# Column sums of a modulation vector: 32x32 block transpositions on VectorE and one matmul per section, in place of ones-matmuls per four columns

## The chip, the cores and the metric

The program runs on one core of a Trainium2 chip, in one launch. The metric is device time in microseconds (us), taken as the median of several executions. One more execution is profiled, and all rows below come from that one. TensorE is called PE here, VectorE DVE, ScalarE ACT, GpSimd POOL, and SyncE, which issues nearly all transfers, SP.

## What is computed

Two transformer-like blocks run one after the other on 512 tokens of width 1024, in float32. Each block makes a modulation vector of 6 sections of 1024 numbers from one condition vector; the sections scale, shift and gate the block's two halves:

```python
mod = (jax.nn.silu(c) @ w_ada[i] + b_ada[i])[:, None, :]
shift_m, scale_m, gate_m, shift_f, scale_f, gate_f = jnp.split(mod, N_MOD, axis=-1)
h = rmsnorm(x, norm_mix_w[i]) * (1.0 + scale_m) + shift_m
x = x + gate_m * hybrid_mixer(h, ...)        # chunked state-space scan, pooling branch, w_out
h = rmsnorm(x, norm_mlp_w[i]) * (1.0 + scale_f) + shift_f
x = x + gate_f * (jnp.square(jax.nn.relu(h @ w_up[i])) @ w_down[i])
...
mod = c_act @ w_ada[l] + b_ada[l]            # second block: six sections again
y = token_mixer(h, ...)                      # mLSTM heads beside banded attention
y = conv_ffn(h, ...)
```

So the modulation is two products of a vector of 1024 with a matrix of 1024 x 6144. Everything else is large products with 512 token rows, and the scan, attention and norms between them.

## The kernel before

**Large products.** Every weight matrix comes from memory in pieces of 128 x 1024 (tile `wraw`). ACT rounds a piece to its high part `whi` (L243), DVE forms the low part `wlo` (L244), and PE multiplies in three fp32r products, high by high, low by high and high by low, with 512 columns each (L274 into `ga`, L352 into `gb`). PE, DVE and ACT each work through one fixed list of instructions. A scheduler writes these lists when the program is built; it takes the order of the Python code as its priority and moves instructions within it. An instruction at the head of an engine's list that waits holds everything behind it.

**The modulation.** It is too thin for PE's large products, so DVE does it, spread over the whole run in small steps. `ada_steps` handles two columns of 128 outputs: two transfers of 512 KB each bring the weights, and eight DVE operations of 128 x 256 (L155, then seven of L157) multiply by the condition's value of each partition and add up into an accumulator `adacc`. What is left is the sum over the 128 partitions. `ada_sum` does this for four columns, that is two accumulators: four fp32 matmuls with a matrix of ones, each into 32 partitions of a PSUM tile `adaps` (L164, eight records in the trace, since an fp32 matmul shows as two), a copy by ACT to `colraw` (L167), a PE transposition (L170), and one DVE addition of the bias into `mod` (L171). Four sections of block 1 and six of block 2, two sums each: 20 such sums. (The first two sections of block 1 have code of their own, `first_mod`, L497 on: two accumulators for each of 8 columns, taken from the same ring of `ADB` buffers as `adacc`, matmuls L506, transposition L511, DVE L512.)

`ada_next` is one step of it. `pump` calls it between the other work at a rate that each stage sets, and `ada_until(block, section)` is called where a section is needed; it finishes what of it is missing. The vectors are needed at these places: (0,2) before the gate rows `gm`, (0,4) and (0,3) before the `w_out` product, (0,5) at the end of the first half of the `w_up` products, where `cols_to_rows` turns it into rows (PE transposition `rowps`, L216, ACT copy L218), (1,0) and (1,1) at the end of the second half, (1,2), (1,4) and (1,3) at the end of the attention and mLSTM stage, and (1,5) before the last `w_down` product (`g2_col`, again `rowps`).

**Stages, by the trace's time.** 0 to 70 us: first norms, `first_mod`, first columns of `w_in` (`h_tile`: `ntmp`, `hh`, `hl`, lines L424 to L433). 190 to 610 us: the state-space scan, where DVE and ACT do the decay tiles and the convolution between products. 650 to 675 us: the `w_out` product and the second norm, tile by tile. 675 to 1020 us: `w_up` and `w_down`. 1020 to 1260 us: mixer of block 2 (`ips`, L1430, and `hm`, L1448, belong to the mLSTM). After 1260 us: its feed-forward part.

## Time and profile before

| | |
|---|---|
| median of 3 executions | 1624.59 us (1624.26 to 1624.70) |
| the profiled execution | 1624.09 us |
| its span, first to last instruction | 1622.3 us |
| PE busy | 1589.5 us |
| DVE busy | 1086.5 us |
| ACT busy | 715.4 us |
| POOL busy | 28.3 us |

The span is what the trace covers; 1.8 us of the execution lie around it. Busy time is the sum of an engine's instructions. Matmuls overlap, so their durations can't be added up: what one costs PE is read from the distance between starts.

### The profile page before, as it was taken

Reading aid. Unit: us, or ns where it says so; the run is one execution under the profiler, and the core shown is the slowest. Engines: PE = TensorE matmul, PEld = TensorE weight load, DVE = VectorE, ACT = ScalarE, POOL = GpSimd, SP = SyncE. Lnnn points to the kernel's source line nnn. Section 1 sums busy time; section 2 is a strip of 40 time slices with the busy share of each in tenths; the row PEclk is TensorE's granted clock in tenths of the full one; section 3 lists DMA queues with packets and bytes.
Section 4 is the critical chain, followed back from the end, with each engine's and each line's share of the span. In section 5 each row is a group of like instructions: output and inputs, shape, how many; then the busy total and the mean of one; then the engine's idle time right before and its main releaser. Section 6 shows DMA issues by size and latency. Waiting matters only on the chain.

```text
span 1622.3 us, 20792 instructions
## 1 busy us (share of the span) xinstructions
PE 1589.5 (98%) x7810; PEld 1274.0 (79%) x7810; DVE 1086.5 (67%) x1995; ACT 715.4 (44%) x1275; POOL 28.3 (2%) x47
## 2 busy tenths in 40 slices
PE   5999999999999999999999999999999999999998
PEld 3778777777877878877877788887788888888886
DVE  6686897888766675876257773578876756145644
ACT  4543656555454332633214332655555643144421
POOL 0000000000000000000000000000011000000000
PEclk9999999999999999999999999999999999999999
DMA  9731544444444435466236571122331323332321
GB/s 280 197 100 59 178 142 149 130 143 138 149 130 138 142 127 177 137 196 209 96 115 197 195 252 48 53 81 76 94 102 53 103 81 102 91 104 87 96 91 53
DMA packets 206830, 206.45 MB, mean 127 GB/s; under 512 B 11469, under 2 KB 184585, under 8 KB 206729
## 3 DMA queue, kind: packets, MB, share of 16 engines
q1 hardware_dynamic: 206729, 205.12, 41.6%
q8 instruction: 61, 1.00, 0.3%
q14 instruction: 40, 0.33, 0.1%
HBM read 202.90 MB, written 2.19 MB: 126 GB/s over the span
## 4 chain that ended last, share of the span: by engine, by line
PE 90%; DVE 4%; DMA 3%; ACT 2%; issue 1%; SPq 0%; POOL 0%; DVEq 0%; POOLq 0%; ACTq 0%
PE ga L274 53%; PE gb L352 21%; PE gb L312 5%; PE go L1494 2%; PE ga L544 2%; DMA wraw<-in_w_ada_dram 1%; DMA AB<-acs 1%; DVE wlo L244 1%; PE nps L424 1%; PE yps L829 1%; PE stps L838 0%; ACT arel L803 0%; PE yps L834 0%; DMA x<-in_x_dram 0%; PE adaps L164 0%
## 5 line engine op out<-in xcount | busy, mean ns | idle before, releaser
L274 PE MATMUL ga<-hh,whi 128*128 128x512 f32 (+1 forms) x1200 | 464.6, 390 | 1.0 <-ACT hh L431 0.9
L244 DVE TENSOR_TENSOR wlo<-wraw,whi 128x1024 fp32r<-128x1024 f32 (+3 forms) x249 | 297.9, 1198 | 246.8 <-ACT whi L243 246.2
L274 PE MATMUL ga<-hl,whi 128*128 128x512 f32 (+1 forms) x1200 | 457.6, 382 | 2.2 <-DVE hl L433 2.1
L274 PE MATMUL ga<-hh,wlo 128*128 128x512 f32 (+1 forms) x1200 | 456.8, 382 | 0.0
L243 ACT ACTIVATE whi<-wraw 128x1024 fp32r<-128x1024 f32 (+3 forms) x249 | 257.5, 1036 | 335.3 <-PE gb L352 151.4
L274 PEld LDWEIGHTS ga<-hh,whi 128*128 128x128 f32 x1200 | 224.1, 188 | 54.1 <-issue 6.7
L274 PEld LDWEIGHTS ga<-hl,whi 128*128 128x128 f32 x1200 | 225.3, 188 | 50.6 <-issue 3.3
L274 PEld LDWEIGHTS ga<-hh,wlo 128*128 128x128 f32 x1200 | 225.3, 188 | 46.7
L157 DVE SCALAR_TENSOR_TENSOR adacc<-wraw,csil,adacc 128x256 f32<-128x256 f32 x280 | 133.7, 482 | 36.1 <-DMA wraw<-in_w_ada_dram 31.7
L352 PE MATMUL gb<-whi,hidh 128*128 128x512 f32 x240 | 78.2, 396 | 0.0
L352 PE MATMUL gb<-wlo,hidh 128*128 128x512 f32 x240 | 77.8, 394 | 0.0
L352 PE MATMUL gb<-whi,hidl 128*128 128x512 f32 x240 | 77.5, 394 | 0.0
L450 DVE SCALAR_TENSOR_TENSOR xs<-xraw,colB,xs 128x511 f32<-128x511 f32 (+2 forms) x72 | 53.8, 748 | 8.8 <-ACT xs L448 7.9
L352 PE MATMUL gb<-whi,fh 128*128 128x512 f32 x176 | 57.3, 396 | 0.0
L352 PE MATMUL gb<-wlo,fh 128*128 128x512 f32 x176 | 57.2, 395 | 0.0
L352 PE MATMUL gb<-whi,fl 128*128 128x512 f32 x176 | 57.0, 394 | 0.0
L352 PEld LDWEIGHTS gb<-whi,hidh 128*128 128x128 f32 x240 | 45.0, 188 | 10.8 <-issue 0.4
L803 ACT ACTIVATE arel<-AB,acs 128x128 f32<-128x128 f32 x128 | 40.7, 389 | 29.0 <-DMA AB<-acs 20.6
L352 PEld LDWEIGHTS gb<-whi,hidl 128*128 128x128 f32 x240 | 45.1, 188 | 10.7
L352 PEld LDWEIGHTS gb<-wlo,hidh 128*128 128x128 f32 x240 | 45.1, 188 | 10.4
L274 PE MATMUL ga<-yh,whi 128*128 128x512 f32 x128 | 51.1, 399 | 0.0
L274 PE MATMUL ga<-yh,wlo 128*128 128x512 f32 x128 | 50.6, 395 | 0.0
(421 smaller groups left out, 2374.2 us busy)
## 6 DMA issues: line engine op xcount, KB each, us to landing
wraw<-in_w_ada_dram SPq DMA_DIRECT2D x80, 512.0 KB
wraw<-in_w_in_dram SPq DMA_DIRECT2D x72, 512.0 KB
wraw<-in_w_down_dram SPq DMA_DIRECT2D x54, 512.0 KB
wraw<-in_w_up_dram SPq DMA_DIRECT2D x88, 256.0 KB
wraw<-in_w_up_dram SPq DMA_DIRECT2D x32, 512.0 KB
araw<-in_w_ada_dram SPq DMA_DIRECT2D x32, 256.0 KB
AB<-acs SPq DMA_DIRECT2D x32, 256.0 KB
wraw<-in_w_branch_ssd_dram SPq DMA_DIRECT2D x16, 512.0 KB
```

Of the source, the lines that this page charges most:

```text
L157: V.scalar_tensor_tensor(out=acc, in0=raw[:, k], scalar=s_, in1=acc, op0=ALU.mult, op1=ALU.add)
L243: act(out=hi, in_=raw, func=AF.Copy)
L244: V.tensor_tensor(out=lo, in0=raw, in1=f(hi), op=ALU.subtract)
L274: PE.matmul(ps[:, n0:n1], lhsT=a[:, m * P:(m + 1) * P], rhs=b[:, n0:n1], start=i == 0, stop=i == 3 * n - 1)
L312: PE.matmul(pss[t][:, 0:ncols], lhsT=a[:, t * P:(t + 1) * P], rhs=b, start=k == 0 and j == 0, stop=k == n - 1 and j == 2)
L352: PE.matmul(pss[t][q], lhsT=a, rhs=w[b][q], start=i == 0 and j == 0, stop=i == n - 1 and j == 2)
L424: PE.transpose(ps[:, i * P:(i + 1) * P], xh[t][j // 4][:, (j % 4) * P:(j % 4 + 1) * P], ident)
L450: V.scalar_tensor_tensor(out=o[:, d:], in0=ps[:, 0:S - d], scalar=cols[taps - 1 - d], in1=o[:, d:], op0=ALU.mult, op1=ALU.add)
L544: PE.matmul(fps[i], lhsT=a[:, i * P:(i + 1) * P], rhs=b, start=j == 0 and q == 0, stop=j == 7 and q == 2)
L803: act(out=t[:, i * P:(i + 1) * P], in_=AB[q][:, i * P:(i + 1) * P], func=AF.Relu, scale=-1.0, bias=acs[:, hh:hh + 1])
L829: PE.matmul(ps[r * 64:(r + 1) * 64, j * P:(j + 1) * P], lhsT=xdt[:, hh * 64:(hh + 1) * 64], rhs=M[hh // 4][:, (hh % 4) * P:(hh % 4 + 1) * ...
L1494: PE.matmul(opss[t][q], lhsT=x_, rhs=w[q][b_], start=half == 0 and k == 0 and j == 0, stop=half == 1 and k == 3 and j == 2)
```

## The change

The accumulator now holds four columns (128 x 512, a tile from the general pool `U` of 64 slots, no longer from the ring of `ADB`). When its 32 operations are done, DVE transposes it in blocks of 32 x 32 (L165, tile `adtr`) and sums each block's rows (L166), which leaves 16 numbers per partition in `adR`: the sums over each group of 32 partitions. When a section is needed, one fp32 matmul with a constant matrix `quarters` (four identity matrices of 32 in each direction) adds the four groups of partitions (L196). Three small DVE operations keep from the four results the one that belongs to each partition (L198, L201) and add the bias (L202). The PE transposition and ACT's copy are gone. `ADB`, now only the ring of `first_mod`, goes from 5 to 3. Two constants are made once. Line numbers above 206 become smaller by 8, those above 590 by 3.

```diff
--- before.py
+++ after.py
@@ -143,36 +143,32 @@
     mod = [const("mod1", [P, 48]), const("mod2", [P, 48])]
     ada_w, bcol = [w_ada, w_ada_2], [ba_col, None]
 
+    adR = [const("adR1", [P, 192]), const("adR2", [P, 192])]
     def ada_steps(ci, col):
 
-        acc = small("adacc", [P, 2 * P], bufs=ADB)
-        for k0 in (0, 4):
-            raw = RAW([P, 4, 2 * P])
-            dma(out=raw, in_=ada_w[ci][0, k0 * P:(k0 + 4) * P, col * P:(col + 2) * P].rearrange("(k p) n -> p k n", p=P))
-            for k in range(4):
-                s_ = csil[:, 8 * ci + k0 + k:8 * ci + k0 + k + 1]
-                if k0 + k == 0:
-                    V.tensor_scalar(out=acc, in0=raw[:, k], scalar1=s_, scalar2=None, op0=ALU.mult)
-                else:
-                    V.scalar_tensor_tensor(out=acc, in0=raw[:, k], scalar=s_, in1=acc, op0=ALU.mult, op1=ALU.add)
-            yield acc
-    def ada_sum(ci, col, accs):
-        ps = PS("adaps")
-        for j in range(4):
-            PE.matmul(ps[j * 32:(j + 1) * 32, 0:P], lhsT=ones[:, 0:32], rhs=accs[j // 2][:, j % 2 * P:(j % 2 + 1) * P],
-                      start=True, stop=True)
-        row = small("colraw", [P, P])
-        act(out=row, in_=ps[:, 0:P], func=AF.Copy)
-        yield
-        ps = PS("adaps")
-        PE.transpose(ps[:, 0:P], row, ident)
-        V.tensor_tensor(out=mod[ci][:, col:col + 4], in0=ps[:, 0:P:32], in1=bcol[ci][:, col:col + 4], op=ALU.add)
-        yield
-    ada_todo = [(0, 8 * sec + i) for sec in (2, 4, 3, 5) for i in range(0, 8, 2)] + [(1, i) for i in range(0, 48, 2)]
-    ada_now, ada_open, ada_half = [], [], []
+        acc = U("adacc")
+        for h in range(2):
+            a = acc[:, h * 2 * P:(h + 1) * 2 * P]
+            for k0 in (0, 4):
+                raw = RAW([P, 4, 2 * P])
+                dma(out=raw, in_=ada_w[ci][0, k0 * P:(k0 + 4) * P, (col + 2 * h) * P:(col + 2 * h + 2) * P].rearrange("(k p) n -> p k n", p=P))
+                for k in range(4):
+                    s_ = csil[:, 8 * ci + k0 + k:8 * ci + k0 + k + 1]
+                    if k0 + k == 0:
+                        V.tensor_scalar(out=a, in0=raw[:, k], scalar1=s_, scalar2=None, op0=ALU.mult)
+                    else:
+                        V.scalar_tensor_tensor(out=a, in0=raw[:, k], scalar=s_, in1=a, op0=ALU.mult, op1=ALU.add)
+                if h and k0:
+                    tr = U("adtr")
+                    V.transpose(out=tr, in_=acc)
+                    V.tensor_reduce(out=adR[ci][:, col * 4:col * 4 + 16], in_=tr.rearrange("p (b f) -> p b f", f=32),
+                                    axis=AX.X, op=ALU.add)
+                yield
+    ada_todo = [(0, 8 * sec + i) for sec in (2, 4, 3, 5) for i in (0, 4)] + [(1, i) for i in range(0, 48, 4)]
+    ada_now = []
     pump_rate = [0, 0]
 
     def pump():
@@ -181,33 +177,29 @@
         if pump_rate[0] and pump_rate[1] % pump_rate[0] == 0:
             ada_next()
 
-    def ada_close(n):
-        while ada_half:
-            next(ada_half.pop(0))
-        while len(ada_open) > max(n, 1):
-            (ci, col), a0 = ada_open.pop(0)
-            ada_half.append(ada_sum(ci, col, (a0, ada_open.pop(0)[1])))
-            next(ada_half[-1])
-        while ada_half and n == 0:
-            next(ada_half.pop(0))
     def ada_next(hold=False):
+        if not ada_now and ada_todo:
+            ci, col = ada_todo.pop(0)
+            ada_now.append([4, (ci, col), ada_steps(ci, col)])
         if ada_now:
-            key, gen = ada_now.pop()
-            ada_open.append((key, next(gen)))
-            return
-        if not hold:
-            ada_close(3)
-        if ada_todo and len(ada_open) < ADB - 1:
-            ci, col = ada_todo.pop(0)
-            ada_now.append(((ci, col), ada_steps(ci, col)))
-            next(ada_now[0][1])
+            next(ada_now[0][2])
+            ada_now[0][0] -= 1
+            if ada_now[0][0] == 0:
+                ada_now.pop()
 
     def ada_until(ci, sec):
-        todo = [(ci, 8 * sec + i) for i in range(0, 8, 2)]
-        while any(t in todo for t in ada_todo + [t for t, _ in ada_now]):
+        todo = [(ci, 8 * sec), (ci, 8 * sec + 4)]
+        while any(t in todo for t in ada_todo + [n[1] for n in ada_now]):
             ada_next()
-        ada_close(0)
+        ps = PS("adaps")
+        PE.matmul(ps[:, 0:32], lhsT=quarters, rhs=adR[ci][:, sec * 32:sec * 32 + 32], start=True, stop=True)
+        own = small("adown", [P, 32])
+        V.tensor_tensor(out=own.rearrange("p (c j) -> p c j", j=4), in0=ps[:, 0:32].rearrange("p (c j) -> p c j", j=4),
+                        in1=quarter.unsqueeze(1).to_broadcast([P, 8, 4]), op=ALU.mult)
+        m = mod[ci][:, 8 * sec:8 * sec + 8]
+        V.tensor_reduce(out=m, in_=own.rearrange("p (c j) -> p c j", j=4), axis=AX.X, op=ALU.add)
+        V.tensor_tensor(out=m, in0=m, in1=bcol[ci][:, 8 * sec:8 * sec + 8], op=ALU.add)
 
     def cols_to_dram(name, col):
 
@@ -589,6 +581,11 @@
     V.tensor_tensor(out=sel, in0=ident[:, 0:32], in1=ident[:, 32:64], op=ALU.add)
     for j in (2, 3):
         V.tensor_tensor(out=sel, in0=sel, in1=ident[:, j * 32:(j + 1) * 32], op=ALU.add)
+    quarters, quarter = const("quarters", [P, P]), const("quarter", [P, 4])
+    V.tensor_copy(out=quarters.rearrange("p (j f) -> p j f", f=32), in_=sel.unsqueeze(1).to_broadcast([P, 4, 32]))
+    V.tensor_reduce(out=quarter, in_=ident.rearrange("p (j f) -> p j f", f=32), axis=AX.X, op=ALU.add)
 
     def xbc_items(g):
 
@@ -1657,8 +1654,8 @@
 OUT_SLOTS = ("M12 M21 W1", "M13 M04 M22 M14 W0", "M31 W2 M32 M23 M33", "", "M24 M34")
 
 UB = 64
+ADB = 3
 SETTLE = (7, 15)
-ADB = 5
 POOLN = 1
 LATE = (3, 4, 0, 4)
 T1TAIL = 5

```

The scheduler's lists change with it. The first place is DVE's list in `first_mod` at the start of the program. The rows are the first steps of the third column and the end of the second: `adacc` are accumulators, `araw` weights, `adaps` the PSUM result; what an instruction waits for stands in brackets. Before:

```order
L500 TENSOR_SCALAR adacc_313<-araw_239,csil_112 128x256 [waits DMAHW1_49,DMAHW0_49]
L500 TENSOR_SCALAR adacc_314<-araw_239,csil_112 128x256
L502 SCALAR_TENSOR_TENSOR adacc_313<-araw_239,csil_112,adacc_313 128x256 [waits DVE_49]
L502 SCALAR_TENSOR_TENSOR adacc_314<-araw_239,csil_112,adacc_314 128x256 [waits DVE_49]
L512 TENSOR_TENSOR mod1_115<-adaps_269,colA_108 128x2 [waits PE_49]
```

The same five instructions in the change:

```order
L492 TENSOR_SCALAR adacc_315<-araw_241,csil_112 128x256 [waits DMAHW1_49,DMAHW0_49]
L492 TENSOR_SCALAR adacc_316<-araw_241,csil_112 128x256 [waits DVE_49,PE_49]
L494 SCALAR_TENSOR_TENSOR adacc_315<-araw_241,csil_112,adacc_315 128x256 [waits DVE_49]
L494 SCALAR_TENSOR_TENSOR adacc_316<-araw_241,csil_112,adacc_316 128x256 [waits DVE_49]
L504 TENSOR_TENSOR mod1_115<-adaps_271,colA_108 128x2 [waits PE_49]
```

Nothing moved, but with a ring of three the second accumulator of a column now waits for PE to have read the first one of the column before.

The second place is DVE's list in the `w_out` stage, at the norm of one token tile, before:

```order
L432 TENSOR_SCALAR ntmp_5817<-nps_5814,gc_f_5430,mod1_115 128x256 [waits Activation_49]
L157 SCALAR_TENSOR_TENSOR adacc_5906<-wraw_6205,csil_112,adacc_5906 128x256 [waits DMAHW3_49]
L433 TENSOR_TENSOR hl_5457<-ntmp_5817,hh_5456 128x256 [waits DVE_49]
L1022 TENSOR_TENSOR tmp_5821<-gb_5470,gm_4731 128x512
L1022 TENSOR_TENSOR tmp_5824<-gb_5471,gm_4733 128x512
L1023 TENSOR_TENSOR x_5444<-x_5444,tmp_5821 128x512 [waits DVE_49]
L1023 TENSOR_TENSOR x_5446<-x_5446,tmp_5824 128x512 [waits DVE_49]
```

And in the change:

```order
L424 TENSOR_SCALAR ntmp_5777<-nps_5774,gc_f_5390,mod1_115 128x256 [waits Activation_49]
L425 TENSOR_TENSOR hl_5417<-ntmp_5777,hh_5416 128x256 [waits DVE_49]
L1019 TENSOR_TENSOR tmp_5781<-gb_5430,gm_4695 128x512
L1019 TENSOR_TENSOR tmp_5784<-gb_5431,gm_4697 128x512
L1020 TENSOR_TENSOR x_5404<-x_5404,tmp_5781 128x512 [waits DVE_49]
L1020 TENSOR_TENSOR x_5406<-x_5406,tmp_5784 128x512 [waits DVE_49]
```

The modulation step that waited for its weights between `ntmp` and `hl` has gone from here; its like stands 25 rows further down.

The third place is PE's list where section (0,5) becomes rows, at the start of the first `w_down` product. Before, from the second group of `gb` on:

```order
L352 MATMUL gb_6779<-whi_6787,hidh_6168 128x512
L352 MATMUL gb_6779<-wlo_6788,hidh_6168 128x512
L352 MATMUL gb_6779<-whi_6787,hidl_6169 128x512
L170 MATMUL adaps_6764<-consts_72,colraw_6762 128x128 [waits Activation_49]
L216 MATMUL rowps_6767<-consts_72,mod1_115 8x128 [waits PE_49]
L352 MATMUL gb_6778<-whi_6787,hidh_6168 128x512 [waits DVE_49]
```

In the change, from the new matmul on:

```order
L196 MATMUL adaps_6695<-adR1_117,quarters_730 128x32
L344 MATMUL gb_6711<-whi_6721,hidh_6130 128x512 [waits Activation_49]
L344 MATMUL gb_6711<-wlo_6722,hidh_6130 128x512 [waits DVE_49]
L344 MATMUL gb_6711<-whi_6721,hidl_6131 128x512
L344 MATMUL gb_6713<-whi_6721,hidh_6130 128x512 [waits Activation_49]
L344 MATMUL gb_6713<-wlo_6722,hidh_6130 128x512
L344 MATMUL gb_6713<-whi_6721,hidl_6131 128x512
L344 MATMUL gb_6715<-whi_6721,hidh_6130 128x512 [waits Activation_49]
L344 MATMUL gb_6715<-wlo_6722,hidh_6130 128x512
L344 MATMUL gb_6715<-whi_6721,hidl_6131 128x512
L344 MATMUL gb_6717<-whi_6721,hidh_6130 128x512 [waits Activation_49]
L208 MATMUL rowps_6701<-consts_72,mod1_115 8x128 [waits DVE_49]
```

`rowps` now stands ten products behind the section's own matmul, and waits for the DVE operations that follow it. In DVE's list these are L198, L201 and L202, with two modulation steps (L162) and the squaring of `relu` (L1051, which waits for ACT) between them:

```order
L198 TENSOR_TENSOR adown_6697<-adaps_6695,quarter_731 128x32 [waits PE_49]
L162 SCALAR_TENSOR_TENSOR adacc_6624<-wraw_6797,csil_112,adacc_6624 128x256 [waits DVE_49]
L1051 TENSOR_TENSOR relu_6688<-relu_6688 128x512 [waits Activation_49]
L201 TENSOR_REDUCE mod1_115<-adown_6697 128x8 [waits DVE_49]
L162 SCALAR_TENSOR_TENSOR adacc_6624<-wraw_6797,csil_112,adacc_6624 128x256 [waits DVE_49]
L202 TENSOR_TENSOR mod1_115<-mod1_115,colA_108 128x8 [waits DVE_49]
```

Before, `rowps` waited for nothing but PE.

## Rows read from the trace of the kernel before

**Rows 1.** The page: busy times, granted clock in 40 slices, chain that ended last.

```profile
PE 1589.5 (98%) x7810; PEld 1274.0 (79%) x7810; DVE 1086.5 (67%) x1995; ACT 715.4 (44%) x1275; POOL 28.3 (2%) x47
...
PEclk9999999999999999999999999999999999999999
...
PE 90%; DVE 4%; DMA 3%; ACT 2%; issue 1%; SPq 0%; POOL 0%; DVEq 0%; POOLq 0%; ACTq 0%
```

**Rows 2.** Windows: stretch, its length, busy time of each engine, clock, DMA.

```profile
190.00:320.00 130.00, 129.30 (x709) 102.64 (x708) 111.62 (x192) 72.58 (x138) 1.93 (x1) 1.00 0.48 145
320.00:440.00 120.00, 120.00 (x628) 95.33 (x627) 98.69 (x168) 63.65 (x114) 1.01 (x1) 1.00 0.47 144
440.00:520.00 80.00, 79.15 (x468) 62.03 (x467) 54.17 (x100) 41.28 (x83) 1.18 (x1) 1.00 0.44 132
520.00:610.00 90.00, 90.00 (x406) 72.38 (x405) 65.67 (x104) 30.84 (x42) 1.01 (x1) 1.00 0.43 135
```

**Rows 3.** Chain of waits, 830 to 890 us: start, length, what.

```profile
829.97 13.26 PE gb L352 x57
843.24 0.36 PE adaps L164 x8
843.59 11.35 PE ga L274 x48
854.94 0.11 PE adaps L170
855.05 11.16 PE ga L274 x48
866.22 0.35 PE adaps L164 x8
```

**Rows 4.** Chain of waits, 600 to 615 us.

```profile
607.26 0.57 PE adaps L164 x16
```

**Rows 5.** Chain of waits at 139 us.

```profile
139.22 0.81 PE dtps L713 x8
```

**Rows 6.** DVE groups by shape: busy and mean ns, idle time before them.

```profile
L244 DVE TENSOR_TENSOR wlo<-wraw,whi 128x1024 fp32r<-128x1024 f32 x233 | 284.8, 1223 | 241.0 <-ACT whi L243 240.4
L157 DVE SCALAR_TENSOR_TENSOR adacc<-wraw,csil,adacc 128x256 f32<-128x256 f32 x280 | 133.7, 482 | 36.1 <-DMA wraw<-in_w_ada_dram 31.7
...
L415 DVE TENSOR_SCALAR nx<-x,nr 128x512 f32<-128x512 f32 x12 | 5.5, 484 | 4.1 <-POOL nr L396 2.1 <-DMA araw<-in_w_ada_dram 1.3 <-DMA wraw<-in_w_in_dram 0.7
...
L1318 DVE TENSOR_REDUCE amx<-sm 128x4 f32<-128x512 f32 x8 | 5.5, 682 | 0.1
```

**Rows 7.** Line L171: duration in ns, least, median and most; first and last start.

```profile
L171 DVE TENSOR_TENSOR mod<-adaps,colC x12: 151/155/164, 707.4 to 1192.0; 128x4 f32<-128x4 f32 x12
L171 DVE TENSOR_TENSOR mod<-adaps,colA x8: 154/158/161, 330.3 to 610.4; 128x4 f32<-128x4 f32 x8
```

**Rows 8.** What PE waited for: us in total, times, longest.

```profile
PE ga L274 <- DVE hl L433: 2.1, 1, 2.1
...
PE nps L424 <- ACT ntmp L428: 0.8, 1, 0.8
...
PE ips L1430 <- DVE mod L171: 0.6, 1, 0.6
```

**Rows 9.** Timeline, 652 to 670 us, all engines; idle time before it in brackets.

```profile
660.69 0.48 DVE L157 SCALAR_TENSOR_TENSOR adacc<-wraw,csil,adacc 128x256 f32<-128x256 f32 x1 [1.75 <-DMA wraw<-in_w_ada_dram]
```

**Rows 10.** Timeline of DVE, 20 to 32 us.

```profile
24.73 0.61 DVE L500 TENSOR_SCALAR adacc<-araw,csil 128x256 f32<-128x256 f32 x2
...
27.38 0.16 DVE L512 TENSOR_TENSOR mod<-adaps,colA 128x2 f32<-128x2 f32 x1 [1.25 <-PE adaps L511]
```

**Rows 11.** Timeline of PE, 20 to 32 us.

```profile
25.91 0.66 PE L506 MATMUL adaps<-adacc,ones 128*64 128x128 f32 x8
```

**Rows 12.** Timeline of PE, 753 to 756 us.

```profile
753.57 0.50 PE L352 MATMUL gb<-whi,hidh 128*128 128x512 f32 x1
```

**Rows 13.** Timeline of ACT, 749 to 757 us.

```profile
754.00 0.58 ACT L1053 ACTIVATE relu<-ga 128x512 f32<-128x512 f32 x1
```

## Prediction

> **What bounds the kernel now.** First the page: PE is busy in 1589.5 us of a span of 1622.3, DVE in 1086.5, ACT in 715.4, and the chain that ended last runs on PE for 90% of the span [rows 1]. The granted clock stands at its upper digit in all 40 slices, so 2.4 GHz is the level before, and nothing here asks PE for less work than it has now; I take the clock as unchanged. PE is the bound, then: a microsecond of matmul taken out is worth a microsecond, as long as PE's list does not run into a wait.
>
> Second, the windows, to see where PE is least sure of that. In the scan stage DVE is at 111.62 of 130 us, 98.69 of 120, 54.17 of 80 and 65.67 of 90, in all 330.2 of 420, while PE stands idle for 1.6 us only [rows 2]. So DVE has little room there, the room is not even, and work added to DVE can turn into PE's waits there and hardly elsewhere. Third, the waits of PE, for the stalls that the new order would add or take away [rows 8].
>
> **PE: what is removed.** A sum's eight records are not worth eight durations, since matmuls overlap. I read its price from starts. From one sum to the next, 843.24 to 866.22, pass 22.98 us, which hold 48 + 48 large matmuls, one sum and one transposition. The large ones alone cost 13.26 / 57 = 0.2326 us each in the piece just before, so 96 of them 22.33. Sum and transposition together cost 0.65 us [rows 3]. The two pieces named after them (0.36 + 0.11) give 0.47; the rest lies in the gap that shows when the next large matmul starts. Twenty times 0.65 is 13.0. Where two sums stand back to back, the sixteen records take 0.57 us and not 2 x 0.36 [rows 3, 4]; there are three such pairs in the trace, so the second sum of each costs some 0.2 to 0.35 less, 0.6 to 1.0 in all. I take **-12.2 us**, with 20 x 0.47 less the 0.6, that is 8.8, and 13.0 as its ends.
>
> **PE: what is added.** One fp32 matmul of 128 x 128 by 32 columns per section, ten in all. The nearest row has this shape: eight records, which are four matmuls, in 0.81 us, 0.20 each [rows 5]. With a little for the switch from and to the large ones I take 0.22, **+2.2 us** (2.0 to 6.5, the upper end being the full price of an old sum).
>
> **DVE: what is added.** Per four columns a transposition of 128 x 512 and a reduction from 128 x 512 to 128 x 16. The trace has no block transposition. Below, it is bounded by the plain one-input operation on the same tile, 484 ns; above, by an operation with twice the elements, 1223 ns. The reduction has a row of its own size, 682 ns. I take 680 for the transposition too, since it reads one float32 tile of the same size in an order that is not plain [rows 6]. Twenty pairs are 20 x 1.36 = 27.3 us (23.3 to 38.1). Each section also brings three small operations at about 155 ns, 30 x 0.155 = 4.7, and twenty bias additions of that size go, -3.1 [rows 7]. DVE gets some 29 us more in 1622, and PE pays for none of it where DVE waits for ACT anyway: its largest group alone stands idle for 241 us in front of its operations [rows 6].
>
> The Trainium skill has a figure that speaks against this. Its page "VectorE: DVE Perf Modes", section "The three transpose paths", gives 311 ns for VectorE's transposition of 128 x 128 in bf16, and section "Rules for kernel authors" calls `tensor_reduce` the slowest operation of this engine, to be restructured. The trace does not agree on the second: 682 ns is no more than other operations of 512 elements take. If the first grows with the elements, 4 x 0.311 = 1.24 us is an estimate for the tile here, DVE's load would be 20 x 0.56 = 11 us larger than my sum has it, and eight of those twenty, 4.5 us, would lie in the scan stage; if PE paid for all of that, the sum below would be 1619 us.
>
> ACT loses twenty copies, which gives PE nothing, as ACT is busy in 44% of the span [rows 1]. The weights' transfers stay the same in number and size, and SP's list shifts only with the steps that they belong to.
>
> **The scan stage, 190 to 610 us.** Eight of the twenty pairs should fall there, since eight of the twenty bias additions lie between 330 and 610.4 us [rows 7]: 8 x 1.36 = 10.9 us on an engine that has 420 - 330.2 = 90 us free. In proportion to the share that is busy, 79%, most of a pair would delay something on DVE; but PE lost only 1.6 us there with all that load, since products stand between. I charge PE for a seventh of it, **+1.5 us**; the ends are 0 and the whole 10.9.
>
> **Waits that go.** In the `w_out` stage one modulation step stood between `ntmp` and `hl`. DVE stood idle for 1.75 us there until its weights came, and then worked on it for 0.48 [rows 9]; PE waited 2.1 us for `hl`, and 0.8 for the next tile's `ntmp` [rows 8]. In the new list that step is further down. What is late next is the transfer's step itself, behind which work for later tiles is queued, so some of the loss may come back. **-2.0 us** (-2.9 to 0). At 1192 us `ips` waited 0.6 us for a bias addition behind the `hm` operations; this goes with L171 [rows 8]: **-0.5 us** (-0.6 to 0).
>
> **Waits that come.** In `first_mod` DVE's second L500 must now wait for the matmuls at 25.91 us, where it ran at about 25.0; behind it are queued two L502 and L512. But DVE idled for 1.25 us in front of L512 [rows 10, 11], which covers the shift for this column; six columns follow with less room. **+0.3 us** (0 to 1.5).
>
> Section (0,5): `rowps` now stands ten products, 10 x 0.2326 = 2.3 us, behind its matmul. Between lie L198, a step of 482 ns, the squaring of `relu`, L201, one more step and L202. The squaring waits for ACT's `relu`, which began 0.43 us after the first `gb` product and took 0.58 [rows 12, 13]. From there: squaring 0.69, L201 0.16, step 0.48, L202 0.16, together 1.5, so L202 ends some 2.5 us after that first product, while `rowps` is due at 2.3; with the hand-over between engines on top I take **+0.6 us** (0 to 1.5). Section (1,5) has only four products, 0.9 us, between its matmul and `rowps`, and four small DVE operations in a row, 4 x 0.155 = 0.6, plus two hand-overs: **+0.4 us** (0 to 1.5).
>
> **The sum.** -12.2 + 2.2 + 1.5 - 2.0 - 0.5 + 0.3 + 0.6 + 0.4 = -9.7 us. From the profiled execution's 1624.09 us that is 1614.4. The median of the runs is 0.5 us above the profiled one, so a median after should be near 1615.
>
> **The rivals.**
>
> *DVE becomes the bound of the scan stage.* The place is 190 to 320 us, where DVE has 18 of 130 us free [rows 2], and the same mechanism up to 610. Price: each of the eight pairs goes whole to PE. Without the scan term the sum is -11.2, so the point from which it decides is 11.2 / 8 = 1.4 us per pair, just what I take a pair to last. With a transposition at the upper end, 1.22 + 0.68 = 1.9, it is 15.2 - 11.2 = +4.0, 1628 us, slower. For it speaks the density of the windows and that the scheduler's list shifts there as a whole; against it, that PE lost almost nothing at that density before. Chance 0.09.
>
> *The sums cost PE less than the starts say, and the new waits take their upper ends.* With 0.47 for each sum with its transposition (8.8), half a pair's time lost in each of the eight (5.4), and 1.0 at each of the two `rowps`: -8.8 + 2.2 + 5.4 - 2.0 - 0.5 + 0.3 + 2.0 = -1.4, 1622.7 us, no difference that shows. For it: in part of the scan stage the chain leaves PE, and a matmul taken out in front of a wait only makes the wait longer. Chance 0.15, with the cases between it and the forecast.
>
> *More is won than the sum says.* The `w_out` wait goes whole (-2.9), the scan stage loses nothing, 13.0 for the sums: -13.0 + 2.2 - 2.9 - 0.6 + 0.3 + 0.6 + 0.4 = -13.0, 1611 us; a scheduler's list that happens to be better in the scan stage adds up to the 1.6 us that PE idles there. Chance 0.16.
>
> **How the numbers follow.** The forecast has 0.60, for 1612 to 1619. Leaving out the slower rival and part of the second, the range for 8 in 10 is 1608 to 1623. About 0.2%, 3.2 us, is what a measurement of this kernel can tell from no change: below 1621.4 is faster. The forecast, the third rival and a little of the second make 0.80; within 0.2% 0.11; slower 0.09.
>
> **What the profile after would show.** No L170, no ACT copy, ten records of the new matmul's line in place of twenty sums; PE's busy time about 10 us less; the chain's large pieces unbroken between 690 and 930 us, at 0.2326 us a product. DVE near 1115 us, the transposition's mean between 484 and 1223 ns. No wait of `ga` for `hl` of 2 us in the `w_out` stage; waits of `rowps` for L202 and for `g2_col` that weren't there, below 1.5 us each. PE's idle time between 190 and 610 us near 3 us. The forecast is wrong if that idle time grows past 8 us, if a transposition takes over 1.2 us, or if the moved modulation steps hold up another tile of the norm stage by as much as they did before.

## The result

The changed kernel takes 1614.29 us (median of 4 runs, 1614.18 to 1614.99) against 1624.64 us before, a ratio of 0.9936 with a 95% interval of 0.9919 to 0.9953. It is faster by some 10 us, 0.6%; 1615.0 was predicted. Its profile has a span of 1612.4 us, 9.9 us less than before; PE's busy time gives 6.4 of it and its idle time 3.5. The page's busy times, clock and chain:

```profile
PE 1583.1 (98%) x7650; PEld 1273.3 (79%) x7650; DVE 1107.2 (69%) x2047; ACT 711.7 (44%) x1255; POOL 27.7 (2%) x47
...
PEclk9999999999999999999999999999999999999999
...
PE 93%; DVE 3%; DMA 2%; ACT 1%; SPq 1%; issue 0%; POOL 0%; DVEq 0%; POOLq 0%; ACTq 0%
```

Against [rows 1] DVE has 20.7 us more, PE 160 records less (180 of the sums go, 20 of the new matmul come), and the chain runs on PE for 93% where it was 90%. The new lines, with least, median and most duration in ns:

```profile
L165 DVE STREAM_TRANSPOSE adtr<-adacc x20: 699/704/711, 248.5 to 928.6; 128x512 f32<-128x512 f32 x20
```

```profile
L166 DVE TENSOR_REDUCE adR<-adtr x20: 671/679/686, 249.7 to 930.4; 128x16 f32<-128x512 f32 x20
```

A pair takes 1.38 us; 1.36 was assumed from the reduction's row [rows 6]. The durations of all DVE instructions add up to 28.4 us more, as foreseen. The page's busy time grows by 20.7 only, since instructions overlap at their ends and the page counts that once. In the scan stage DVE's load rises where [rows 2] showed it, and PE's idle time falls:

```profile
190.00:320.00 130.00, 129.61 (x703) 102.03 (x703) 110.41 (x188) 73.56 (x139) 1.94 (x1) 1.00 0.45 134
320.00:440.00 120.00, 120.00 (x619) 96.32 (x618) 105.98 (x182) 64.38 (x115) 1.01 (x1) 1.00 0.51 155
440.00:520.00 80.00, 80.00 (x454) 63.71 (x453) 55.90 (x103) 41.20 (x79) 1.01 (x1) 1.00 0.43 130
520.00:610.00 90.00, 90.00 (x396) 72.92 (x395) 69.58 (x118) 30.84 (x41) 1.01 (x1) 1.00 0.47 149
```

DVE is at 341.9 of 420 us, 11.7 more than before, and PE idles for 0.4 us where it idled for 1.6. In the `w_out` stage, 640 to 680 us, PE's waits are now these, in place of the 2.1 and 0.8 us of [rows 8]:

```profile
PE ga L266 <- DVE hl L425: 0.3, 1, 0.3
PE nps L416 <- DVE ntmp L424: 0.2, 1, 0.2
```

And where section (0,5) becomes rows, the chain of waits shows no step between the ten products and `rowps`, L208, so the wait foreseen there is not to be seen:

```profile
668.61 76.63 PE ga L266 x370
745.23 0.14 PE adaps L196 x2
745.38 2.42 PE gb L344 x10
747.80 0.11 PE rowps L208
```

**Where the time came from.** Both kernels run the same 7630 other PE records, so each can be found in both traces. The table gives how much later (+) or earlier (-) they start than in the profile of the kernel before, as the median over the records in the 10 us from the named time on (time of the trace before), in us. The rows below the first belong to the experiments.

```
kernel                 180 us    640 us    680 us   1060 us   1240 us   1560 us
changed                 +2.0      -2.8      -6.1     -11.6     -12.1      -9.9
after_again             +0.3      -4.1      -7.4     -13.0     -11.9      -9.7
after_shift64           +2.3      -2.3      -5.5     -10.6     -11.0      -8.8
after_ring5             +1.4      -1.8      -5.0     -10.9      -9.8      -9.1
after_dve2              +1.7      -2.6      -2.7      -8.7      -9.1      -7.2
after_pe_sums           +1.7      +2.0      -1.3      -0.3      -0.5      -0.4
before_no_sums          +0.6      -1.8      -1.6      -8.3      -7.4      -6.5
before_wout_free        +1.2      +1.5      +2.4      +1.3      +4.0      +5.5
before_wout_free2       +1.2      +1.9      -0.8      -2.5      +4.9      +9.2
```

The changed kernel loses 2.0 us in the first stage, wins 4.8 in the scan, 3.2 in `w_out`, 5.6 in `w_up` and `w_down` and 0.5 in the mixer of block 2, and gives 2.2 back after 1240 us, where nothing of the modulation is left but one section. That last item was in no one's sum, neither the forecast's nor a rival's.

One thing differs between these profiles that their pages don't show, since a slice of 40 us prints a 9 for anything from 0.9 on: the granted clock. In the kernel before, the changed kernel, after_shift64 and after_pe_sums the trace's records have it at the upper level from 29 us at the latest to within 5 us of the end. In the others it is at 0.50, the lower level (1.2 GHz), for one short stretch or three: after_again from 1076.0 to 1079.4 us, after_ring5 from 1078.6 to 1082.0, after_dve2 from 669.6 to 673.0, before_wout_free from 668.8 to 672.2, before_wout_free2 from 1256.3 to 1259.7, and before_no_sums three times, from 500.0 to 503.5, 660.5 to 663.9 and 1080.3 to 1083.7. What that costs stands with the experiments.

### The profile page after: what moved, and what is told of

It reads as the page before. It is cut to its first block, busy times and chain, and to the rows that moved or that the text cites. A ratio compares the mean times of both kernels' runs of the same rounds, so it can differ in the third digit from the quotient of the medians.

```text
span 1612.4 us, 20493 instructions
## 1 busy us (share of the span) xinstructions
PE 1583.1 (98%) x7650; PEld 1273.3 (79%) x7650; DVE 1107.2 (69%) x2047; ACT 711.7 (44%) x1255; POOL 27.7 (2%) x47
## 4 chain that ended last, share of the span: by engine, by line
PE 93%; DVE 3%; DMA 2%; ACT 1%; SPq 1%; issue 0%; POOL 0%; DVEq 0%; POOLq 0%; ACTq 0%
PE ga L266 56%; PE gb L344 21%; PE gb L304 5%; PE go L1491 2%; PE ga L536 1%; PE yps L826 1%; PE stps L835 1%; PE yps L831 1%; DMA wraw<-in_w_ada_dram 1%; PE nps L416 1%; DMA araw<-in_w_ada_dram 1%; SPq L109 1%; DVE wlo L236 0%; PE xtps L787 0%; DMA x<-in_x_dram 0%
## 5 line engine op out<-in xcount | busy, mean ns | idle before, releaser
L162 DVE SCALAR_TENSOR_TENSOR adacc<-wraw,csil,adacc 128x256 f32<-128x256 f32 x280 | 130.2, 480 | 17.0 <-DMA wraw<-in_w_ada_dram 14.4
```

The costliest lines, as they stand in the source:

```text
L162: V.scalar_tensor_tensor(out=a, in0=raw[:, k], scalar=s_, in1=a, op0=ALU.mult, op1=ALU.add)
```

## The experiments

The theory was that PE's time in the sums is the gain, that the `w_out` wait adds to it, and that DVE has room for the new work. The rivals were that DVE binds the scan stage, that removed sums only lengthen other waits, and that the freed accumulators and the new order made the gain. All kernels were timed beside the kernel before, each group on one chip.

**The changed kernel again**, unedited.

> The changed kernel once more, unedited. Its first profile shows two things that no edited instruction explains: large products start every 0.2333 us between 1250 and 1550 us where the kernel before has 0.2311, and before 27 us PE runs products at a spacing of 0.43 us for 1 us longer. If these belong to one execution, a second profile has them elsewhere or not at all and the span differs by some 1 to 3 us; if they belong to the program as built, the second profile repeats them within 0.3 us. Time 1614 us either way.

1614.88 us (5 runs), ratio 0.9936 (0.9923 to 0.9948). The products after 1250 us are again 0.2333 us apart, so that belongs to the program as built. The 2.0 us of the first stage do not: here the lag at 180 us is 0.3. The timeline of PE shows what differs, by one product of the same run of six, in the first profile and in this one:

```profile
25.94 0.63 PE L536 MATMUL ga<-hl,whi 128*128 128x512 f32 x1
```

```profile
25.12 0.40 PE L536 MATMUL ga<-hl,whi 128*128 128x512 f32 x1
```

In the first the products stand 0.43 us apart for all six, in the second only for the first two; the program is the same. Between 1060 and 1240 us this execution in turn loses 1.1 us. There the granted clock (third number from the end; columns as in [rows 2]) is at its lower level:

```profile
1076.10:1079.40 3.30, 3.30 (x8) 2.58 (x9) 3.30 (x14) 1.96 (x10) 0.00 (x0) 0.50 0.02 5
```

Products of 512 columns start 0.43 us apart in this stretch, and the lead shrinks by 1.6 us. From 1070.4 us until the clock fell PE ran mostly small matmuls of 4 to 128 columns; the first profile has the same list there and no such stretch.

**The ring of the first sections.**

```diff
-UB = 64
-ADB = 3
+UB = 63
+ADB = 5
```

> The changed kernel with a ring of five buffers for the first two sections' accumulators, as before, paid for with one slot of the general pool (63 for 64). Theory: the ring of three costs PE 0.4 us at 31 us, and the rest of the 2.1 us that the changed kernel is behind at 70 us is the clock and the transfers; then the lead at 70 us changes by -0.4 to -1 us, and the time by no more than 1 us, if the missing slot does no harm. Rival: the ring is the whole cause, directly and by way of the products' spacing that follows a longer idle stretch; then 2.1 us come back, 1612.2 us.

1614.42 us (5 runs), ratio 0.9929 (0.9916 to 0.9941), no difference from the changed kernel. The timeline of PE at the product that waits for the second column's `hh`, first with the ring of three, then with five:

```profile
31.19 0.49 PE L536 MATMUL ga<-hh,whi 128*128 128x512 f32 x1 [0.89 <-ACT hh L421]
```

```profile
30.85 0.50 PE L536 MATMUL ga<-hh,whi 128*128 128x512 f32 x1 [0.54 <-ACT hh L421]
```

The kernel before waits 0.47 us at this place. All other profiles with a ring of three show 0.87 to 0.89. So the ring costs 0.3 to 0.4 us, and the rival, that it made all of the 2.1 us, is out: after_again has the ring too and lags by 0.3 only. This edit also moves the pools of tiles, and the late products are 0.2317 us apart with it: it gives back 0.7 us after 1240 us, not 2.2.

**The kernel before without sums.** The edit in `ada_sum`; the bias is added to the accumulators as they stand:

```diff
-        ps = PS("adaps")
-        for j in range(4):
-            PE.matmul(ps[j * 32:(j + 1) * 32, 0:P], lhsT=ones[:, 0:32], ...)
-        row = small("colraw", [P, P])
-        act(out=row, in_=ps[:, 0:P], func=AF.Copy)
         yield
-        ps = PS("adaps")
-        PE.transpose(ps[:, 0:P], row, ident)
-        V.tensor_tensor(out=mod[ci][:, col:col + 4], in0=ps[:, 0:P:32], ...)
+        for i in range(2):
+            V.tensor_tensor(out=mod[ci][:, col + 2 * i:col + 2 * i + 2], in0=accs[i][:, 0:2 * P:P], ...)
```

> The kernel before without the sums over partitions: the four ones-matmuls, the copy and the transposition of each of the twenty sums are left out, and two small DVE additions per sum take one partition's part as it stands. The accumulators, their ring and the modulation steps stay. The wait in the stage of w_out stays in DVE's list too. If the sums cost PE what the starts say, this gives -12.2 us, with the small wait at 1192 us -12.8, 1612 us. Rival: only the 9.4 us that the pieces of the chain name as theirs, or less since part of them filled waits, 1615 to 1619 us.

1617.63 us (5 runs), ratio 0.9951 (0.9939 to 0.9964): 7.7 us won, not 12.2. The price of a sum is right all the same where products stand without gaps: between 820 and 940 us, where six of the twenty lie, the lead grows by 3.9 us, 0.65 each. In the scan stage eight sums are gone and only 2.4 us won; PE's two waits there grew, on the same two tiles:

```profile
PE yps L828 <- DVE st L838: 1.2, 1, 1.2
PE xtps L784 <- DVE xs L452: 1.1, 1, 1.1
```

They were 0.85 and 0.70 us long before. Taking sums out alone does in part what the second rival said: some of it, 0.8 us here, turns into waits for DVE. More went to the clock. This profile has three stretches at the lower level, the first behind the wait of 1.2 us, the second behind the `w_out` wait, 2.4 us long here, the third behind small matmuls:

```profile
500.10:503.40 3.30, 3.22 (x29) 2.89 (x29) 2.40 (x5) 0.68 (x2) 1.92 (x1) 0.50 0.31 67
660.50:663.80 3.30, 3.30 (x18) 3.30 (x17) 3.30 (x10) 1.98 (x6) 0.00 (x0) 0.50 0.21 75
1080.40:1083.70 3.30, 3.30 (x11) 2.50 (x9) 3.30 (x14) 2.21 (x11) 0.00 (x0) 0.50 0.00 0
```

Beyond the longer waits, the lead shrinks by 1.3 us over the first, 0.2 over the second and 1.6 over the third. The profile of the kernel before has none of them. So the 7.7 us are not the worth of the sums alone. In the profile the lead is 7.4 us at 1240 us; with 3.1 for the clock and 0.8 for the two waits the estimate is 11.3, near the 12.2. All five executions show a mean granted clock of 0.996 or 0.997, those of the kernel before beside them 0.997 to 0.999, so the clock has a share in the medians too, though a smaller one.

**The changed kernel with the old sums.** The accumulators of four columns stay in the general pool; at their end stands the old sum, one step later:

```diff
-                    tr = U("adtr")
-                    V.transpose(out=tr, in_=acc)
-                    V.tensor_reduce(out=adR[ci][:, col * 4:col * 4 + 16], ...)
+                    ada_half.append(ada_sum(ci, col, acc))
...
     def ada_next(hold=False):
+        ada_flush(1)
...
-        PE.matmul(ps[:, 0:32], lhsT=quarters, rhs=adR[ci][:, sec * 32:sec * 32 + 32], start=True, stop=True)
-        ...
+        while ada_half:
+            ada_flush(1)
```

> The changed kernel with its four-column accumulators in the general pool and its ring of three, but with the old sums: for each four columns four ones-matmuls, ACT's copy, PE's transposition and the bias addition, a step later each; no transposition by DVE, no matmul per section. Theory: the PE time of the sums is the gain, so this gives back 20 x 0.65 less the 2.2 of the ten matmuls, 10 to 11 us, where all of it is on the path: 1625 us. From the kernel without sums, which won 7.7 us and not 12.2, a second figure: 7.7 - 2.2 = 5.5 us given back, 1620 us. Rival: the freed ring and the order of the steps made the gain, and it stays at 1615 to 1616 us.

1625.28 us (11 runs), ratio 0.9995 (0.9986 to 1.0004): all is given back. In the same group of runs the changed kernel's lists (after_shift64, below) took 1614.13 us, so the sums' way of being made is worth 11.2 us by the medians. By the spans of single profiles, none of which has the clock fall, it is 9.4 against the changed kernel and 8.3 against after_shift64. The rival of the freed ring falls. But the table shows one thing that stays: from 640 to 680 us this kernel wins 3.3 us too. The `w_out` gain comes with the new accumulators and the order of their steps, not with the transposition. That the whole is still no faster than before has no single cause in the table: it loses 2.0 us up to 640 us and 0.8 between 680 and 1240 us, and why was not tried.

**DVE's new work twice.**

```diff
                     V.transpose(out=tr, in_=acc)
+                    V.tensor_reduce(out=adR[ci][:, col * 4:col * 4 + 16], ...)
+                    V.transpose(out=tr, in_=acc)
                     V.tensor_reduce(out=adR[ci][:, col * 4:col * 4 + 16], ...)
```

> The changed kernel with DVE's transposition and reduction done twice for each four columns: 20 x 1.38 = 27.7 us more on DVE, eight of them, 11 us, in the scan stage. Theory: DVE has room, PE pays for a small part, +0 to +3 us, 1614 to 1618 us. Rival: the scan stage is bound by DVE, +11 us, 1625 us.

1617.39 us (5 runs), ratio 0.9947 (0.9936 to 0.9960), 3.3 us above after_shift64 in the same group. The scan stage pays next to nothing: it wins 4.3 us where the changed kernel wins 4.8, with DVE at 350.6 of 420 us. Two of the four windows, to be read against those of the result:

```profile
320.00:440.00 120.00, 120.00 (x620) 96.28 (x619) 107.62 (x186) 63.88 (x115) 1.18 (x1) 1.00 0.50 156
440.00:520.00 80.00, 80.00 (x455) 63.68 (x454) 58.42 (x107) 41.30 (x79) 1.01 (x1) 1.00 0.43 129
```

PE pays in two other places, by its waits between 640 and 780 us:

```profile
PE nps L419 <- DVE ntmp L427: 2.1, 1, 2.1
PE rowps L211 <- DVE mod L205: 0.7, 1, 0.7
```

In the chain of waits the pair and its repetition stand in front of an `ntmp` of the last norm of the `w_out` stage, one after the other, with modulation steps between:

```profile
663.82 0.62 DVE adtr L165
664.44 0.23 DVE adacc L160
664.67 0.60 DVE adR L166
665.27 0.39 DVE adacc L162
665.66 0.62 DVE adtr L168
666.28 0.37 DVE adacc L162
666.65 0.60 DVE adR L169
667.25 0.39 DVE adacc L162
667.64 0.47 DVE ntmp L427
```

Behind that wait of 2.1 us the granted clock is at its lower level:

```profile
669.60:672.90 3.30, 3.30 (x17) 3.29 (x16) 3.30 (x10) 1.33 (x4) 0.00 (x0) 0.50 0.38 129
```

Products of 256 columns start 0.21 us apart in it, and 0.12 behind it. So of the 3.1 us that the `w_out` stage loses against the changed kernel, 2 are the longer wait and 1 is the clock. The transposition is free as long as it does not stand in a norm's chain; the changed kernel has one pair at this place, and PE waits 0.5 us in the stage. The rival that DVE binds the scan stage is out.

**The `w_out` wait by itself**, in the kernel before. Two trials. The step inside the product is skipped, and `pump` begins again at the group of `w_up` with number 3, then 5:

```diff
-            if i < n - tail and (i % 2 or n == 16):
+            if i < n - tail and (i % 2 or n == 16) and (script is None or script.__name__ != "script1"):
                 ada_next(True)
...
-    pump_rate[0] = 1
+    pump_rate[0] = 0
...
+            if half == 0 and q == 3:
+                pump_rate[0] = 1
```

> The kernel before with the modulation's steps held back in the stage of w_out: the step inside that product is left to a later call, and the pump starts again two column groups later in w_up. The step that waited for its weights between ntmp and hl is gone from there and stands behind the next tile's additions. Theory: PE's waits of 2.1 and 0.8 us go, -2 to -3.2 us, 1621.4 to 1622.6 us. Rival: the same wait comes up at the next tile's norm, since the weights come no earlier, and the time is the same within 1 us.

1628.06 us (11 runs), ratio 1.0015 (1.0006 to 1.0024): slower. PE's waits in the stage, 640 to 680 us, are as long as they were:

```profile
PE ga L274 <- DVE hl L433: 2.0, 1, 2.0
PE nps L424 <- ACT ntmp L428: 0.7, 1, 0.7
```

The timeline of DVE shows why. The next step stands behind the tile's additions, in front of the next norm, and waits for its weights there, longer than the 1.75 us of [rows 9]:

```profile
665.94 0.35 DVE L155 TENSOR_SCALAR adacc<-wraw,csil 128x256 f32<-128x256 f32 x1 [2.62 <-DMA wraw<-in_w_ada_dram]
```

The rival was right for this edit: the wait moved. That the stage loses 0.9 us, from +1.5 to +2.4, is the clock, which fell behind the wait of 2.0 us and did not fall behind the 2.1 us of the kernel before:

```profile
668.90:672.20 3.30, 3.15 (x15) 2.80 (x14) 1.12 (x3) 2.31 (x6) 0.00 (x0) 0.50 0.50 159
```

The rest of the loss comes later, 2.7 us between 1060 and 1240 us, where modulation steps now run until 1138 us (until 958 us in the kernel before), and 1.5 us after that. The second trial:

> The kernel before with the modulation held back further: no step inside the product of w_out, and the pump starts again five column groups into w_up. No modulation step stands in DVE's list between the first and the last norm of this stage; the next one stands 31 rows behind the last pair of additions. Theory: a step that waits for its weights cost the 3.2 us here, and the first trial only moved it to the next tile; now PE's idle time in the stage falls from 3.2 to under 0.6 us, and the lead at 690 us is -2.7 to -3.2. The steps put off come later, at the end of the second half of w_up, where they may cost up to 2 us: 1621 to 1624 us. Rival: the norms themselves are late, and PE's idle time stays near 3 us.

PE's waits in the stage are down to one:

```profile
PE nps L424 <- ACT ntmp L428: 0.8, 1, 0.8
```

The stage wins 2.7 us, from +1.9 to -0.8. The whole is 1633.31 us (5 runs), ratio 1.0044 (1.0030 to 1.0057), much worse than expected: the steps put off pile up in the mixer of block 2, where they run until 1250 us, and the lead of 2.5 us at 1060 us becomes a lag of 4.9 at 1240 and 8.3 at 1260. The clock has a part in the last step: it fell at 1256.3 us, behind a wait of 1.6 us. So a step that waits for its weights is what cost 2.7 of the 3.2 us, and holding the steps back is no way to have them. PE still idles for 0.9 us in the stage, where under 0.6 was expected.

**The spacing of the products after 1250 us.** First all tiles moved together, by 64 unused bytes in front of the general pool:

```diff
-    adR = [const("adR1", [P, 192]), const("adR2", [P, 192])]
+    shift = const("shift", [P, 16]); adR = [const("adR1", [P, 192]), const("adR2", [P, 192])]
```

> The changed kernel with an unused constant of 64 bytes per partition in front of the general pool, so that every tile behind it lies 64 bytes further; no engine's list changes. Question: the start-to-start spacing of the large products after 1250 us, 0.2333 us here and 0.2311 in the kernel before, with a pattern of 24 values that repeats. If it hangs on where the operands lie against some boundary, the pattern changes and the time with it, by up to 3 us either way; if it hangs on the tiles' distances from each other, or on the order of instructions, the pattern stays, 1614.3 to 1614.9 us.

1614.13 us (5 runs), ratio 0.9926 (0.9914 to 0.9938). The pattern stays value for value. Then the same unused bytes between the general pool, where the token operands lie, and the pool of the weights, 32, 64 and 128 of them (the edit for 128):

```diff
-    up = ctx.enter_context(tc.tile_pool(name="up", bufs=UB))
+    up = ctx.enter_context(tc.tile_pool(name="up", bufs=UB)); gp = ctx.enter_context(tc.tile_pool(name="gp", bufs=1)); gp.tile([P, 32], F32, tag="gap", name="gap")
     wp = ctx.enter_context(tc.tile_pool(name="wp", bufs=WB))
```

> The changed kernel with an unused 32 bytes per partition between the general pool, which holds the token operands of the large products, and the pool of the weights; the engines' lists stay but for a local shuffle. Question: whether the spacing of the large products after 1250 us, 0.2333 us, hangs on where weights lie against tokens. If it does, the pattern of 24 values changes in one of the three gaps of 32, 64 and 128 bytes, and the mean moves within 0.229 to 0.236; over 1300 products that is -5 to +4 us. If not, the pattern stays and the time is 1614 us.

> The same with 64 bytes between the two pools. As for the gap of 32 bytes: pattern and mean of the spacing change if the weights' place against the tokens counts, and stay at 0.2333 us if it doesn't.

> The same with 128 bytes between the two pools. As for the gap of 32 bytes.

The local shuffle that the first of these speaks of was one of tile numbers; PE's list is the same in all three. The chain's longest piece after 1400 us, 528 products without a gap, in the changed kernel, after_shift64 and the gaps of 32, 64 and 128 bytes, in this order:

```profile
1420.50 123.17 PE ga L266 x528
```

```profile
1421.66 123.17 PE ga L266 x528
```

```profile
1423.90 122.75 PE ga L266 x528
```

```profile
1422.02 122.87 PE ga L266 x528
```

```profile
1421.75 122.20 PE ga L266 x528
```

The kernel before needs 122.04 us for the same piece:

```profile
1431.83 122.04 PE ga L274 x528
```

So the spacing in the late stage changes with the distance between the pools and not with a common shift. That the place of tiles against each other is also what moved it between the kernel before and the changed one is the likely reading, but no run shows it by itself. The gaps ran on a third chip, without the changed kernel's own profile there; on the two chips of after_again and after_shift64 its pattern was the same within 1 ns. For the time it is no lever: the three gaps take 1615.55, 1614.99 and 1614.26 us (4 runs each, ratios 0.9940, 0.9940 and 0.9935). What they win late goes elsewhere. The scan stage wins 3.6 to 4.2 us in their profiles and 4.8 in the changed kernel's, the clock falls in all three between 1077 and 1083 us, and between 650 and 750 us the mean distance of products is 0.2324 us in the changed kernel and 0.2336 with 64 bytes.

## Why the prediction was right

**The sums, -12.2 + 2.2 = -10.0 us.** Right in size. Putting them back into the changed kernel costs 11.2 us by medians and 8.3 to 9.4 by single profiles. The price of 0.65 per sum, read from the distance of starts [rows 3], holds where it was read: 3.9 us for six. The new matmul costs what the row of `dtps` [rows 5] said: in the chain above its two records take 0.14 us, and in the timeline the second product behind it starts another 0.09 us late, 0.23 in all. Taken out of the kernel before, without the new order, the sums gave only 7.7 us; the rest went into two longer waits and into the clock, which fell three times. The forecast reckoned with such waits in a rival, and took the clock as unchanged.

**DVE in the scan stage, +1.5 us.** Too high; the measured charge is nothing. The stage wins 4.8 us, the eight sums less three new matmuls are worth about 4 by the forecast's own prices, and PE's idle time fell by 1.2. A second set of pairs, 11 us more of DVE, cost 0.5. The pair's duration was right to 2%: 704 ns for the transposition, near the reduction's 679, so the choice of the value for the unknown operation held. The Trainium skill's figure on the page "VectorE: DVE Perf Modes", section "The three transpose paths", from which 1.24 us was estimated, does not carry over; the trace decides for 0.70.

**`w_out`, -2.0 us.** The mechanism was right and the size low: -3.2, all of it, past the end of -2.9 that the range of this term had. Nothing came back, because no modulation step stands in this part of the list at all until the last norm. The gain belongs to the order that came with the accumulators (after_pe_sums has it without the transposition), and it is a matter of where a step falls: two edits by hand moved the wait or paid for it elsewhere.

**`first_mod`, +0.3 us.** The ring costs 0.3 to 0.4. The rest of the 2.0 us by which the profile lags there varies from one execution to the next: the lag is 0.3 to 2.9 us in eight profiles with this ring, and 0.6 to 1.2 in three of the kernel before with edits elsewhere, so the profile before was itself an early one. What varies is when the early products change their pace (last section).

**`rowps`, +0.6 and +0.4 us.** Wrong. Neither wait is in the trace of the changed kernel. The estimate put L202's end 2.5 us after the first `gb` product and 0.2 us behind the due time; it came after 2.1 us, and `rowps` ran at 2.4. The small operations cost DVE less in a row than their durations, as they overlap: L201 and the step behind it start 0.09 and 0.40 us before what follows them, for 0.18 and 0.48. It is a close thing: after_shift64 waits 0.35 us there, and with DVE's work doubled the wait is 0.7.

**`ips`, -0.5 us.** The wait went, and another of 0.5 us came in the same stage (`cps` for `vw`, 1182 us); net nothing.

**The clock, taken as unchanged.** It was, in the two profiles compared, from 27.3 us to within 5 us of the end. It was not in the first stage, and another execution of the same program (after_again) lost 1.6 us by it at 1076 us.

**What the sum didn't have:** +2.2 us after 1240 us, by the spacing of products. With these and the first stage's lag PE's busy time fell by 6.4 us, where the prediction had about 10. The terms that were too low (`rowps`, scan stage, `w_out`) are worth some 4 us of gain more than forecast, and this, the first stage and `ips` took back as much. That the total was hit within 1 us is in part luck of that kind.

## What to carry to other kernels

Price a small matmul in a dense stream from the distance of starts around it, not from its duration, and expect the price to hold only where the engine has no wait close by. DVE operations that belong to a side job cost next to nothing at 80% load here where they didn't stand in front of a norm or another chain that PE waits for; the same pair at that one place cost 3.1 us, two thirds of it as a longer wait and one third by the clock behind the wait. When a trial wins less than it should, look for the granted clock in windows of a few us before blaming the waits: the page's slices are too long for it. A step that waits for a transfer inside a fixed list is worth looking for by name, since its move can win more than the edit at hand.

## What was not expected of the hardware

**The distance between equal products is a property of the build.** Products of 512 columns in one stream repeat a pattern, 24 values long in this stage, for hundreds of products. The first 24 distances in ns after 1440 us:

```
changed          235 234 230 228 231 230 229 235 234 227 228 234 254 234 235 237 228 233 232 237 233 234 233 235
shift of 64      237 233 234 233 235 235 234 230 228 231 230 229 235 234 227 228 234 254 234 235 237 228 233 232
gap of 128       230 235 231 235 230 230 234 230 227 236 235 230 233 230 230 231 229 231 228 230 230 228 236 234
kernel before    231 231 226 229 230 238 226 230 233 234 225 234 224 231 226 234 238 232 234 231 233 234 235 228
```

The second row is the first, begun five products earlier. Between 224 and 254 ns lie 13%, and means of 0.2311 to 0.2333 us make 2 to 3 us over the late stage, as much as some terms of the sum. What in the distance of the tiles sets a value stays open.

**The early products run at half pace for a varying time.** At the start of `first_mod` products stand 0.43 us apart and then 0.23, while the page's row of the clock shows its upper digit and the window from 20 to 28 us a granted clock of 1.00 in both kernels. The change of pace came at 24.8 us before, at 26.9 in the first profile of the changed kernel and at 24.6 in the second. The trace's records of the granted clock begin close to these times, at 24.95, 27.23 and 24.72 us, and begin at the upper level; for the time ahead of them there is no record, and the view prints 1.00. So a 1.00 at the start of a program is no reading. Over the eight profiles with the ring of three the records begin between 24.7 and 28.6 us, and the lag at 180 us is 0.3 us in the earliest and 2.3 to 2.9 in the two latest. Why the change came when it did was not tried.

**A wait of PE can cost more than its length.** In nine of the thirteen profiles the granted clock is at 0.50 for one stretch or three between 500 and 1260 us. PE had waited 1.2 to 2.4 us shortly before in five of these stretches, and had run mostly small matmuls in the other six. In such a stretch products of 512 columns start 0.43 us apart and those of 256 columns 0.21, in place of 0.23 and 0.12; a stretch cost 0.9 to 1.6 us where a wait of the kernel before did not make up for it. The length of the wait alone does not settle it: the clock fell behind 1.2 us in before_no_sums and stayed behind 2.1 in the kernel before.
